# A feed-forward layer's norms, closings and second-product operands, moved and split into smaller steps

## The chip, the core and the metric

The kernel runs on one core of a Trainium2 chip. The metric is the time of one execution on the device, in microseconds; smaller is better. TensorE is called PE here, VectorE DVE, ScalarE ACT, GpSimd POOL, and SyncE SP; SP issues all DMAs.

## The reference

One layer of a hybrid encoder over two sequences, 1024 and 512 tokens of width 1024, in float32: a feed-forward block, a mixer (Hyena convolutions and retention), and a second feed-forward block. Both feed-forward blocks are

```python
h = rmsnorm(x, pre_g)
x = x + 0.5 * rmsnorm((silu(h @ w1) * (h @ w3)) @ w2, post_g)
```

with `rmsnorm(x, g) = x * rsqrt(mean(x * x) + 1e-6) * g` over the 1024 features and an inner width of 2816. Only these two blocks are touched by the change; the mixer between them is not.

## The kernel before

**Layout.** Activations lie transposed, features on the 128 partitions and tokens along the free dimension. The 1536 tokens are two halves `g` of 768, each half two quarters `th` of 384. The 1024 features are two groups `kh` of four blocks of 128. A *quad* is a tile of 128 x 4 x 384: one feature group of one quarter. Quads come from a pool `Y` of 20 slots, and operands of the first product also from a pool `X` of 6.

**Split products.** Every float32 operand is split into a high part (`hi_act`, L58, a copy on ACT to the matmul's format) and a low part (`lo`, L61, a subtraction on DVE). `mm3` (L64) then issues three matmuls (L67 to L69). Both feed-forward products use seven block products in place of eight (a Strassen form over `kh` and `th`).

**First product.** `up_unit` (L265) makes one of 22 blocks of 128 inner features for both quarters: four weight tiles of 256 KB by DMA into a ring of five (`raw`), sums of them on DVE (`s0` to `s3`), seven products of 12 matmuls each into three banks (`ua`, `ub`, `uc`), 84 matmuls a block; split weights sit in a ring of ten (`fw`, L279). ACT copies the first bank to `p1` (L291) before the same bank takes the next product, and applies Silu. The results are the `hid` quads, 12 of them by the end. The moving operands (`self.b`, L263) are split once for each half in `operands` (L241); eight of their quads stay in `Y` for the whole first product.

**Second product.** `down` (L336) runs seven forms `p` over `hid`, each in three parts `c` of four, four and three blocks. For each block it makes the moving operand (`bs`, `xh`, `xl`, L357 to L369: a sum of two `hid`, its high and low parts, or a whole quad at once where the form has a single term), loads 256 KB of weights (L370), splits them and issues 48 matmuls, 12 for each of four banks. After a form its banks are added into the four `z` quads (`ev`, L343). The weights of five forms are sums of two blocks of `w2`; `weight_sums` (L321) forms them beforehand in 20 steps (two loads, an add on DVE, a store to `ws`).

**Norms.** `normed` (L215) loads a quarter's two quads, and `sum_sq` (L185) squares them on ACT and adds them up on DVE to `acc`. `rstd3` (L200) sums over partitions with six instructions on PE (`ss`, L205) and takes the reciprocal root: one DVE operation (L94), a power on POOL (L95), four DVE operations (L96 to L100). `spread` (L208) transposes the result into a bank (`rps`, L212). Then eight `scalar_tensor_tensor` on DVE (L233) multiply by the norm weight (one for each partition) and by `rps`. For the second feed-forward's first half the root is not computed there but read from a row that the mixer left (`rq`, L228).

**Closing.** `post_quads` (L399) does the same for the result `z`, eight multiplies on DVE (L413), then adds the input (`res`, loaded at L411) in pairs of blocks (L415) and stores (L416). In the first feed-forward it then sums the squares of the new values and stores their root to a row for the mixer (L418 to L422).

**Order.** Steps that run beside the products are generators. `ahead` (L455) is the norm of half 1 and the weight sums; it runs beside the 22 blocks of half 0. The closing of half 0 runs beside the blocks of half 1. `ffn` (L424) takes steps only between blocks:

```python
                    self.up_unit(w13[f], [hid[fh, th][c][:, i] for th in range(2)])
                    if f:
                        run(beside, 2 if g or f % 2 else 1)
```

and takes all that are left at block 19. In half 1 the closing takes a step after each part of form 6, the last; its remaining steps (`self.rest`) run beside the mixer's first product or, in the second feed-forward, at the kernel's end. The source order is not the order on the engines: the program is laid out by a planner which, by its own model of time, gives each engine the earliest-written instruction that it takes to be ready, and which makes a tile wait until its slot is free. Each engine then runs its instructions strictly in that order.

Of the kernel before, what the change touches and what calls it, by code (L numbers as in the profile page):

```python
# [46 lines left out]
class Kern:  # L47
# [137 lines left out]
    def sum_sq(self, xs, pool):  # L185

        nc = self.nc
        acc = self.half("acc")
        for i, x in enumerate(xs):
# [3 lines left out]
            if i:  # L193
                nc.vector.tensor_tensor(acc, sq[:, 0], acc, ALU.add)
                nc.vector.tensor_tensor(acc, sq[:, 1], acc, ALU.add)
            else:
                nc.vector.tensor_tensor(acc, sq[:, 0], sq[:, 1], ALU.add)
# [16 lines left out]

    def normed(self, src, gi, pool, row, xs):  # L215
# [6 lines left out]
        if row is None:  # L222
            acc = self.sum_sq(xs, pool)
            yield
            r = self.spread(self.rstd3(acc))
        else:
            r = self.half("rq")
            nc.sync.dma_start(r, row.broadcast_to([128, 384]))  # L228
        yield
        for kh in range(2):  # L230
            for k in range(4):
                g = self.gains[:, gi, 4 * kh + k:4 * kh + k + 1]
                nc.vector.scalar_tensor_tensor(xs[kh][:, k], xs[kh][:, k], g, r, ALU.mult, ALU.mult)  # L233
# [7 lines left out]
    def operands(self, load, X, Y):  # L241
# [3 lines left out]
        b = {}  # L245
        h11, h12 = load(0, 0), load(0, 1)
        b["11"] = self.split(X, h11, "b11")
# [17 lines left out]
    def up_unit(self, w13, hid):  # L265
# [36 lines left out]
        tt(u3, bb, p1, ALU.add)  # L302
        product(bc, s[0], "t1", True)
# [32 lines left out]
    def down(self, w2, hid, Y, z, order):  # L336
# [15 lines left out]
        for p in order:  # L352
            old = {7: 1, 6: 3}.get(p)
            (a, *am), (b, *bm) = self.FORMS[p]
            ps = banks[p] = banks[old] if old else [self.bank("dn") for _ in range(4)]
            for c in range(3):
                n = 4 if c < 2 else 3  # L357
                xh, xl = self.quad(Y, "xh", F32R), self.quad(Y, "xl", F32R)
                if not bm:
                    self.hi_act(xh[:, :n], hid[b][c][:, :n])  # L360
                    self.lo(nc.vector, xl[:, :n], hid[b][c][:, :n], xh[:, :n])
                for i in range(n):
                    f = 4 * c + i
                    if bm:
                        t = self.half("bs")
                        tt(t, hid[b][c][:, i], hid[bm[0]][c][:, i], ALU.add if bm[1] > 0 else ALU.subtract)
                        self.hi_act(xh[:, i], t)
                        self.lo(nc.vector, xl[:, i], t, xh[:, i])
                    raw = self.fr.tile([128, 512], F32, tag="raw", name="raw2")  # L369
                    nc.sync.dma_start(raw, self.ws[p][f // 3][:, f % 3 * 512:f % 3 * 512 + 512] if am else w2[a[0], a[1]][:, f * 512:f * 512 + 512])  # L370
                    wh = self.fw.tile([128, 4, 128], F32R, tag="w", name="w2h")
                    wl = self.fw.tile([128, 4, 128], F32R, tag="w", name="w2l")
                    raw = raw.rearrange("p (m c) -> p m c", c=128)
                    self.hi_act(wh, raw)
                    self.lo(nc.vector, wl, raw, wh)
                    for m in range(4):
                        self.mm3(ps[m], wh[:, m], wl[:, m], xh[:, i], xl[:, i], f == 0 and not old, f == 10, old is not None)
                if c < 2:
                    yield p, c
# [19 lines left out]
    def post_quads(self, z, src, dst, gi, Y, row, g, ths=(0, 1)):  # L399
# [3 lines left out]
        for th in ths:  # L403
            acc = self.sum_sq([z[0, th], z[1, th]], Y)
            yield
            r = self.spread(self.rstd3(acc, True))
            yield
            for mh in range(2):
                t = z[mh, th]
                o = self.quad(Y, "res")  # L410
# [839 lines left out]
```

## Time and profile before

| | |
|---|---|
| median of 3 executions | 3393.17 us (3390.63 to 3396.44) |
| profiled execution: time | 3399.09 us |
| its span, first to last instruction | 3397.3 us |
| mean granted TensorE clock | 0.959 of full speed |
| busy: PE, DVE, ACT, POOL | 91%, 78%, 42%, 16% |
| instructions | 46267, of which 16792 matmuls |
| DMA | 485 MB, 143 GB/s over the span |

The first feed-forward takes the span's first 1110 us: its half 0 about 32 to 572 us, its half 1 to 1072 us. The mixer follows to about 2347 us, and the second feed-forward to the end, its half 0 from 2357 to about 2902 us. A busy share is of the whole span. A row of the timeline or of a group gives an engine's instructions, their busy time, and in brackets or behind the bar the idle time of that engine just before them with what ended it.

### The profile page before, as it was taken

How to read it: one execution, taken by the hardware profiler on the slowest of the kernel's cores; microseconds unless marked ns; L12 is line 12 of the kernel's file. 1: busy time of each engine (PE TensorE's matmuls, PEld its weight loads, DVE VectorE, ACT ScalarE, POOL GpSimd, SP SyncE). 2: the span in 40 equal slices, each digit the busy share in tenths (PEclk: the TensorE clock that was granted, in tenths of full speed). 3: DMA queues.
4: the chain of work that ended last, by engine and by line, in shares of the span. 5: the costliest groups of instructions: out<-in, count | busy, mean ns of one | idle time of the engine just before them, and what ended most of it. 6: DMA issues, size and time to landing. Idle time of an engine off the chain costs nothing. (4 is left out here: it accounts for less than half of the span.)

```text
span 3397.3 us, 46267 instructions
## 1 busy us (share of the span) xinstructions
PE 3087.7 (91%) x16792; PEld 2885.7 (85%) x16792; DVE 2644.2 (78%) x4316; ACT 1431.3 (42%) x2373; POOL 555.3 (16%) x400
## 2 busy tenths in 40 slices
PE   5999998999897799989897998984899999999996
PEld 4999998999897677767676887763899999999996
DVE  8788788777877599678655878886888788877776
ACT  4333464333444234355543344332433455333453
POOL 0000000000200323365322544552000000000000
PEclk8999999999998899999998999997999999999998
DMA  3567454322344534453453125454377544422343
GB/s 128 211 232 286 123 156 143 84 72 75 103 131 139 169 117 160 150 172 112 120 173 128 44 83 172 153 172 139 127 266 272 190 147 134 143 72 72 87 128 131
DMA packets 218806, 485.34 MB, mean 143 GB/s; under 512 B 36432, under 2 KB 64464, under 8 KB 216400
## 3 DMA queue, kind: packets, MB, share of 16 engines
q1 hardware_dynamic: 218576, 482.37, 43.3%
q8 instruction: 132, 2.16, 0.3%
q14 instruction: 98, 0.80, 0.1%
HBM read 382.60 MB, written 99.65 MB: 142 GB/s over the span
## 5 line engine op out<-in xcount | busy, mean ns | idle before, releaser
L68 PE MATMUL dn<-xl,w2h 128*128 128x384 f32 x1232 | 414.8, 337 | 12.7 <-DVE xl L62 12.7
L59 ACT ACTIVATE wh<-raw 128x512 fp32r<-128x512 f32 (+1 forms) x312 | 216.6, 694 | 446.0 <-PE ua L68 96.4
L59 ACT ACTIVATE wh<-s 128x512 fp32r<-128x512 f32 x352 | 221.7, 631 | 427.7 <-PE ua L68 122.3
L69 PE MATMUL dn<-xh,w2l 128*128 128x384 f32 x1232 | 392.4, 337 | 0.0
L67 PE MATMUL dn<-xh,w2h 128*128 128x384 f32 x1232 | 386.8, 337 | 1.7 <-ACT xh L59 1.6
L59 ACT ACTIVATE w2h<-raw 128x512 fp32r<-128x512 f32 (+1 forms) x348 | 236.6, 682 | 342.4 <-PE dn L68 214.9
L62 DVE TENSOR_TENSOR wl<-s,wh 128x512 fp32r<-128x512 f32 x352 | 241.8, 688 | 168.5 <-PE ub L68 84.2
L95 POOL TENSOR_TENSOR r<-m,mhalf 128x3 f32<-128x3 f32 (+1 forms) x35 | 38.8, 1108 | 1847.8 <-DVE m L94 1846.9
L62 DVE TENSOR_TENSOR w2l<-raw,w2h 128x512 fp32r<-128x512 f32 (+1 forms) x316 | 219.5, 705 | 126.0 <-ACT w2h L59 107.7
L67 PE MATMUL wips<-hh,wh 128*128 128x512 f32 x576 | 231.9, 403 | 17.7 <-ACT wh L59 16.7
L68 PEld LDWEIGHTS dn<-xl,w2h 128*128 128x128 f32 x1232 | 232.5, 189 | 15.3 <-DVE xl L62 15.3
L67 PEld LDWEIGHTS dn<-xh,w2h 128*128 128x128 f32 x1232 | 229.5, 189 | 3.8 <-ACT xh L59 3.3
L69 PE MATMUL wips<-hh,wl 128*128 128x512 f32 x576 | 230.7, 401 | 1.8 <-POOL wl L62 1.2
L68 PE MATMUL wips<-hl,wh 128*128 128x512 f32 x576 | 230.8, 401 | 0.0
L69 PEld LDWEIGHTS dn<-xh,w2l 128*128 128x128 f32 x1232 | 230.5, 189 | 0.0
L62 DVE TENSOR_TENSOR wl<-raw,wh 128x512 fp32r<-128x512 f32 (+1 forms) x276 | 199.0, 721 | 39.9 <-ACT wh L59 37.9
L67 PE MATMUL fw<-th,mh 128*128 128x256 f32 x448 | 132.3, 297 | 30.9 <-DVE spec L839 18.2
L67 PEld LDWEIGHTS wips<-hh,wh 128*128 128x128 f32 x576 | 110.4, 192 | 46.3 <-ACT wh L59 17.6
L67 PE MATMUL ua<-b11h,wh 128*128 128x384 f32 x352 | 123.7, 351 | 26.6 <-ACT b11h L59 26.6
L69 PEld LDWEIGHTS wips<-hh,wl 128*128 128x128 f32 x576 | 110.3, 192 | 30.0 <-POOL wl L62 2.4
L68 PE MATMUL fw<-tl,mh 128*128 128x256 f32 x448 | 132.3, 296 | 1.3 <-DVE tl L62 1.2
L69 PE MATMUL fw<-th,ml 128*128 128x256 f32 x448 | 130.1, 291 | 3.8 <-POOL ml L62 3.0
(342 smaller groups left out, 9088.9 us busy)
## 6 DMA issues: line engine op xcount, KB each, us to landing
raw<-ffn_w SPq DMA_DIRECT2D x440, 256.0 KB, 2.7
raw<-ws SPq DMA_DIRECT2D x220, 256.0 KB, 2.6
wsum<-ffn_w SPq DMA_DIRECT2D x60, 768.0 KB, 7.5
raw<-w_in_f SPq DMA_DIRECT2D x48, 512.0 KB, 4.3
ws<-wsum SPq DMA_DIRECT2D x30, 768.0 KB, 4.2
xq<-x SPq DMA_DIRECT2D x16, 768.0 KB, 7.2
res<-x SPq DMA_DIRECT2D x16, 768.0 KB, 6.3
raw<-w_out SPq DMA_DIRECT2D x24, 512.0 KB, 3.4
```

The source lines that it names most:

```text
L59: self.nc.scalar.activation(hi, src, AF.Copy)
L62: eng.tensor_tensor(lo, src, hi.bitcast(F32), ALU.subtract)
L67: mm(ps, lhsT=ah, rhs=bh, start=first, stop=False, **kw)
L68: mm(ps, lhsT=ah, rhs=bl, start=False, stop=False, **kw)
L69: mm(ps, lhsT=al, rhs=bh, start=False, stop=last, **kw)
L95: nc.gpsimd.tensor_tensor(r, m, self.mhalf[:, :n], ALU.pow)
```

## The change

The gains of a norm are multiplied in by eight copies on ACT, in place, before the root is known (`gained`); DVE then multiplies by the root alone, a quad (norms) or half a quad (closings) at a time. Sum, root and spread of a norm or closing are steps of their own, and `up_unit` takes one step in its middle (`mid`) and `ffn` one at its end. At the start both quarters' sums, roots and spreads are issued before either is scaled, and the first quarter's first operand is split before the second quarter is scaled. `down` makes the moving operand of a part one part ahead. In half 1 the closing starts one part earlier, at the end of form 5, the sum of squares of `z[0, 1]` is made after the first part of form 6, and a closing's `res` is loaded with its sum.

```diff
@@ -182,17 +182,19 @@
     def half(self, name):
         return self.ft.tile([128, 384], F32, tag="t", name=name)
-    def sum_sq(self, xs, pool):
-
-        nc = self.nc
-        acc = self.half("acc")
+    def sum_sq(self, xs, pool, acc=None):
+
+        nc = self.nc
+        first = acc is None
+        if first:
+            acc = self.half("acc")
         for i, x in enumerate(xs):
             sq = self.quad(pool, "sq")
             nc.scalar.activation(sq, x, AF.Square)
             nc.vector.tensor_tensor(sq[:, 0:2], sq[:, 0:2], sq[:, 2:4], ALU.add)
-            if i:
+            if i or not first:
+                nc.vector.tensor_tensor(sq[:, 0], sq[:, 0], sq[:, 1], ALU.add)
                 nc.vector.tensor_tensor(acc, sq[:, 0], acc, ALU.add)
-                nc.vector.tensor_tensor(acc, sq[:, 1], acc, ALU.add)
             else:
                 nc.vector.tensor_tensor(acc, sq[:, 0], sq[:, 1], ALU.add)
         return acc
@@ -211,6 +213,12 @@
         for t in range(3):
             self.nc.tensor.transpose(ps[:, t * 128:(t + 1) * 128], r[:, t:t + 1].broadcast_to([128, 128]), self.ident)
         return ps
+
+    def gained(self, xs, gi):
+
+        for i in range(8):
+            x = xs[i // 4][:, i % 4]
+            self.nc.scalar.activation(x, x, AF.Copy, scale=self.gains[:, gi, i:i + 1])
     def normed(self, src, gi, pool, row, xs):
@@ -222,15 +230,17 @@
         if row is None:
             acc = self.sum_sq(xs, pool)
             yield
-            r = self.spread(self.rstd3(acc))
+            self.gained(xs, gi)
+            r = self.rstd3(acc)
+            yield
+            r = self.spread(r)
         else:
+            self.gained(xs, gi)
             r = self.half("rq")
             nc.sync.dma_start(r, row.broadcast_to([128, 384]))
         yield
-        for kh in range(2):
-            for k in range(4):
-                g = self.gains[:, gi, 4 * kh + k:4 * kh + k + 1]
-                nc.vector.scalar_tensor_tensor(xs[kh][:, k], xs[kh][:, k], g, r, ALU.mult, ALU.mult)
+        for x in xs:
+            nc.vector.tensor_tensor(x, x, r.unsqueeze(1).broadcast_to([128, 4, 384]), ALU.mult)
     def split(self, pool, src, name):
         h, l = self.quad(pool, f"{name}h", F32R), self.quad(pool, f"{name}l", F32R)
@@ -238,13 +248,14 @@
         self.lo(self.nc.vector, l, src, h)
         return h, l
-    def operands(self, load, X, Y):
+    def operands(self, load, X, Y, first=None):
         tt = self.nc.vector.tensor_tensor
-        b = {}
+        b = first or {}
         h11, h12 = load(0, 0), load(0, 1)
-        b["11"] = self.split(X, h11, "b11")
+        if not first:
+            b["11"] = self.split(X, h11, "b11")
         t1 = self.quad(Y, "t1")
         tt(t1, h12, h11, ALU.subtract)
         yield
@@ -262,7 +273,7 @@
         b["22"] = self.split(Y, h22, "b22")
         self.b = b
-    def up_unit(self, w13, hid):
+    def up_unit(self, w13, hid, mid):
         nc = self.nc
@@ -300,6 +311,7 @@
         product(bb, s[2], "t3", False)
         u3 = self.half("u3")
         tt(u3, bb, p1, ALU.add)
+        mid()
         product(bc, s[0], "t1", True)
         tt(u3, bc, u3, ALU.add)
         product(bb, a22, "t4", False)
@@ -349,34 +361,44 @@
                 else:
                     tt(z[q][:, m], z[q][:, m], ps[m], ALU.add if sign > 0 else ALU.subtract)
-        for p in order:
+        def moving(p, c):
+            _, (b, *bm) = self.FORMS[p]
+            n = 4 if c < 2 else 3
+            xh, xl = self.quad(Y, "xh", F32R), self.quad(Y, "xl", F32R)
+            if not bm:
+                self.hi_act(xh[:, :n], hid[b][c][:, :n])
+                self.lo(nc.vector, xl[:, :n], hid[b][c][:, :n], xh[:, :n])
+            for i in range(n if bm else 0):
+                t = self.half("bs")
+                tt(t, hid[b][c][:, i], hid[bm[0]][c][:, i], ALU.add if bm[1] > 0 else ALU.subtract)
+                self.hi_act(xh[:, i], t)
+                self.lo(nc.vector, xl[:, i], t, xh[:, i])
+            return xh, xl
+
+        parts = [(p, c) for p in order for c in range(3)]
+        ahead = moving(*parts[0])
+        for j, (p, c) in enumerate(parts):
             old = {7: 1, 6: 3}.get(p)
-            (a, *am), (b, *bm) = self.FORMS[p]
-            ps = banks[p] = banks[old] if old else [self.bank("dn") for _ in range(4)]
...
-                if c < 2:
-                    yield p, c
+            a, *am = self.FORMS[p][0]
+            if c == 0:
+                ps = banks[p] = banks[old] if old else [self.bank("dn") for _ in range(4)]
+            xh, xl = ahead
+            for i in range(4 if c < 2 else 3):
+                f = 4 * c + i
+                raw = self.fr.tile([128, 512], F32, tag="raw", name="raw2")
+                nc.sync.dma_start(raw, self.ws[p][f // 3][:, f % 3 * 512:f % 3 * 512 + 512] if am else w2[a[0], a[1]][:, f * 512:f * 512 + 512])
+                wh = self.fw.tile([128, 4, 128], F32R, tag="w", name="w2h")
+                wl = self.fw.tile([128, 4, 128], F32R, tag="w", name="w2l")
+                raw = raw.rearrange("p (m c) -> p m c", c=128)
+                self.hi_act(wh, raw)
+                self.lo(nc.vector, wl, raw, wh)
+                for m in range(4):
+                    self.mm3(ps[m], wh[:, m], wl[:, m], xh[:, i], xl[:, i], f == 0 and not old, f == 10, old is not None)
+            if j + 1 < len(parts):
+                ahead = moving(*parts[j + 1])
+            if c < 2:
+                yield p, c
+                continue
             if p == 1:
                 ev((1, 1), ps, True)
             elif p == 4:
@@ -401,17 +423,20 @@
         nc = self.nc
         for th in ths:
-            acc = self.sum_sq([z[0, th], z[1, th]], Y)
+            acc = self.sum_sq([z[1, th]], Y, z["sum"]) if th and "sum" in z else self.sum_sq([z[0, th], z[1, th]], Y)
+            os = [self.quad(Y, "res") for _ in range(2)]
+            for mh in range(2):
+                nc.sync.dma_start(os[mh], src[mh][th])
+            self.gained([z[0, th], z[1, th]], gi)
             yield
-            r = self.spread(self.rstd3(acc, True))
+            r = self.rstd3(acc, True)
+            yield
+            r = self.spread(r)
             yield
             for mh in range(2):
-                t = z[mh, th]
-                o = self.quad(Y, "res")
-                nc.sync.dma_start(o, src[mh][th])
-                for k in range(4):
-                    nc.vector.scalar_tensor_tensor(t[:, k], t[:, k], self.gains[:, gi, 4 * mh + k:4 * mh + k + 1], r, ALU.mult, ALU.mult)
+                t, o = z[mh, th], os[mh]
                 for k in range(0, 4, 2):
+                    nc.vector.tensor_tensor(t[:, k:k + 2], t[:, k:k + 2], r.unsqueeze(1).broadcast_to([128, 2, 384]), ALU.mult)
                     nc.vector.tensor_tensor(t[:, k:k + 2], t[:, k:k + 2], o[:, k:k + 2], ALU.add)
                     nc.sync.dma_start(dst[mh][th][:, k:k + 2], t[:, k:k + 2])
             if row is not None:
@@ -446,10 +471,14 @@
         with pool("xq", 6, side=side) as X, pool("fs", side=side) as self.fs, pool("ft", 6, side=side) as self.ft, \
                 pool("fw", 10, side=side) as self.fw, pool("fr", 5, side=side) as self.fr, pool("pm", 8, space=PSUM) as self.pm:
             h = [], []
-            for th in range(2):
-                for _ in ready(0, th, h[th]):
-                    pass
-            for _ in self.operands(lambda kh, th: h[th][kh], X, Y):
+            steps = [ready(0, th, h[th]) for th in range(2)]
+            for _ in range(1 if row_in else 3):
+                for step in steps:
+                    next(step)
+            run(steps[0], 9)
+            first = {"11": self.split(X, h[0][0], "b11")}
+            run(steps[1], 9)
+            for _ in self.operands(lambda kh, th: h[th][kh], X, Y, first=first):
                 pass
             def ahead():
@@ -477,9 +506,9 @@
                     for th in range(2):
                         if i == 0:
                             hid.setdefault((fh, th), []).append(self.quad(Y, "hid"))
-                    self.up_unit(w13[f], [hid[fh, th][c][:, i] for th in range(2)])
+                    self.up_unit(w13[f], [hid[fh, th][c][:, i] for th in range(2)], lambda: run(beside, 1 if f else 0))
                     if f:
-                        run(beside, 2 if g or f % 2 else 1)
+                        run(beside, 1)
                 z = {}
                 post_of = self.post_quads(z, srcs[g], dsts[g], post, Y, row_out, g)
                 if g == 0:
@@ -491,7 +520,9 @@
                     beside = post_of
                 else:
                     for p, c in self.down(w2, hid, Y, z, (1, 4, 7, 2, 3, 5, 6)):
-                        if p == 6:
+                        if (p, c) == (6, 0):
+                            z["sum"] = self.sum_sq([z[0, 1]], Y)
+                        if p == 6 or (p, c) == (5, 2):
                             run(post_of)
         self.rest = post_of
```

## Rows read from the trace of the kernel before

**Rows 1.** The page, busy time, share of the span, instructions; PE.

```profile
PE 3087.7 (91%) x16792; PEld 2885.7 (85%) x16792; DVE 2644.2 (78%) x4316; ACT 1431.3 (42%) x2373; POOL 555.3 (16%) x400
```

**Rows 2.** Busy time by stretch: PE, PEld, DVE, ACT, POOL, PEclk, DMA share, GB/s.

```profile
60.00:130.00 70.00, 59.46 (x319) 59.06 (x318) 53.89 (x101) 25.30 (x40) 2.34 (x2) 0.88 0.41 143
130.00:345.00 215.00, 215.00 (x1240) 214.87 (x1240) 183.61 (x287) 82.86 (x149) 0.00 (x0) 1.00 0.73 269
...
560.00:630.00 70.00, 56.23 (x301) 54.99 (x300) 60.84 (x116) 27.34 (x39) 3.40 (x3) 0.88 0.42 140
...
870.00:930.00 60.00, 49.63 (x259) 48.06 (x258) 47.72 (x74) 26.13 (x48) 17.00 (x8) 0.91 0.40 114
...
2395.00:2460.00 65.00, 53.19 (x291) 52.44 (x290) 51.19 (x97) 24.23 (x37) 1.97 (x2) 0.92 0.42 153
...
2895.00:2945.00 50.00, 45.20 (x263) 43.88 (x262) 48.02 (x92) 18.91 (x31) 2.92 (x2) 1.00 0.53 190
```

**Rows 3.** Waits of PE over the span: us in total, times, longest.

```profile
PE ss L205 <- DVE acc L195: 52.1, 8, 13.4
PE rps L212 <- DVE r L100: 33.7, 10, 4.8
...
PE dn L68 <- DVE xl L62: 12.7, 8, 4.2
```

**Rows 4.** Timeline, first feed-forward, closing of half 0: ACT and PE.

```profile
588.15 4.23 ACT L191 ACTIVATE sq<-z 128x1536 f32<-128x1536 f32 x3 [0.86 <-DVE z L415]
...
592.28 0.47 ACT L291 ACTIVATE p<-ua 128x384 f32<-128x384 f32 x1
...
592.81 0.69 PE L67 MATMUL ua<-b21h,wh 128*128 128x384 f32 x1 [7.78 <-ACT p L291]
```

**Rows 5.** Groups by shape, ACT: a copy with a scale per partition, one without, Square.

```profile
L837 ACT ACTIVATE spec<-fw,turn 128x256 f32<-128x256 f32 x104 | 42.1, 475 | 58.7 <-PE fw L69 58.4
L291 ACT ACTIVATE p<-ua 128x384 f32<-128x384 f32 x88 | 41.8, 475 | 20.7 <-PE ua L69 20.7
...
L191 ACT ACTIVATE sq<-z 128x1536 f32<-128x1536 f32 x24 | 34.8, 1478 | 41.1 <-DVE z L415 29.2 <-DVE z L350 10.3 <-issue 1.5
```

**Rows 6.** Timeline, start of the first feed-forward: PE and DVE.

```profile
26.57 1.44 PE L205 MATMUL ss<-ones,acc 128*128 128x1 f32 x6 [6.04 <-DVE acc L195]
...
32.19 4.29 DVE L233 SCALAR_TENSOR_TENSOR xq<-xq,gains,rps 128x384 f32<-128x384 f32 x8 [0.99 <-PE rps L212]
...
36.39 1.75 DVE L249 TENSOR_TENSOR t<-xq 128x1536 f32<-128x1536 f32 x1
```

**Rows 7.** Timeline, start of the second feed-forward: ACT and DVE.

```profile
2346.76 0.63 ACT L59 ACTIVATE wh<-raw 128x512 fp32r<-128x512 f32 x1 [22.77 <-DMA x<-z]
...
2353.47 8.55 DVE L233 SCALAR_TENSOR_TENSOR xq<-xq,gains,rq 128x384 f32<-128x384 f32 x16 [3.55 <-DMA rq<-row]
```

**Rows 8.** Timeline, the kernel's end: PE and DVE.

```profile
3369.91 2.12 DVE L350 TENSOR_TENSOR z<-z,dn 128x384 f32<-128x384 f32 x4 [1.87 <-PE dn L69]
...
3371.27 0.49 PE L212 MATMUL rps<-ident,r 128*128 128x128 f32 x3
3371.94 4.28 DVE L413 SCALAR_TENSOR_TENSOR z<-z,gains,rps 128x384 f32<-128x384 f32 x8
...
3377.01 0.95 DVE L192 TENSOR_TENSOR sq<-sq 128x768 f32<-128x768 f32 x1
...
3381.07 0.56 DVE L195 TENSOR_TENSOR acc<-sq,acc 128x384 f32<-128x384 f32 x1
...
3381.68 1.44 PE L205 MATMUL ss<-ones,acc 128*128 128x1 f32 x6 [9.93 <-DVE acc L195]
...
3390.25 3.56 DVE L415 TENSOR_TENSOR z<-z,res 128x768 f32<-128x768 f32 x4
```

**Rows 9.** Timeline, end of the first feed-forward: PE.

```profile
1084.48 1.44 PE L205 MATMUL ss<-ones,acc 128*128 128x1 f32 x6 [12.52 <-DVE acc L195]
```

**Rows 10.** Busy time in the stretch with the most DMA, columns as in rows 2.

```profile
250.00:280.00 30.00, 30.00 (x175) 30.00 (x174) 26.66 (x41) 11.65 (x22) 0.00 (x0) 1.00 0.99 374
```

More of the change, by code (lines that the diff above doesn't have):

```diff
@@ L350, in ev @@
                     tt(z[q][:, m], z[q][:, m], ps[m], ALU.add if sign > 0 else ALU.subtract)
-        for p in order:
-            old = {7: 1, 6: 3}.get(p)
-            (a, *am), (b, *bm) = self.FORMS[p]
-            ps = banks[p] = banks[old] if old else [self.bank("dn") for _ in range(4)]
[L356 to L377, printed above, removed]
-                if c < 2:
-                    yield p, c
```

## The prediction

> **What bounds the kernel now.** I read four views in this order: the page's busy shares, the busy time by stretch, the waits of PE, and the timeline round the longest of them. The page shows TensorE busy for 91% of the span [rows 1], which says little by itself. The stretches tell more [rows 2]. From 130 to 345 us, the products of a feed-forward half, PE is busy 215.00 of 215.00 us with 1240 matmuls: 215 / 1240 = 0.1734 us each, and nothing beside it can make that faster. DVE is at 85% there and ACT at 39%. So only what PE loses in the other stretches can be won: idle time, and matmuls that ran slowly after idle time. The mean granted clock is 0.88 in 60 to 130 us, where PE had been idle, and 1.00 in 130 to 345 us; 2.4 GHz is the upper of its two levels, 1.2 GHz the lower. A stretch's slow part is its busy time less its matmuls at 0.1734 us.
>
> The waits name the causes [rows 3]: 52.1 us for the sum of squares (`acc`), 33.7 us for the reciprocal root (`r`), 12.7 us for `xl`; the timeline adds one of 7.78 us for ACT's copy of a bank [rows 4]. The first two are chains of a few short instructions that PE, in its fixed order, stands still for, because the sum, the root and the spread follow each other within one block.
>
> All terms below are against the profiled execution, 3399.1 us (span 3397.3); it lies 5.9 us above the median of the runs, 3393.2, so I take the sum off the median.
>
> **Part 1, norms of the second half under the first half's products: -25 us.** The two stretches are 60 to 130 and 2395 to 2460 us. Idle: 70 - 59.46 = 10.5 and 65 - 53.19 = 11.8 us. Slow: 59.46 - 319 x 0.1734 = 4.1 and 53.19 - 291 x 0.1734 = 2.7 us [rows 2]. After the change sum, root and spread are half a block apart: 84 matmuls a block, 42 x 0.1734 = 7.3 us. PE's longest wait for `r` is 4.8 us [rows 3], so 7.3 us of products cover it. Bounds: 0 to -29.1. I take all but 1.5 us of idle time in each, with the slow part in proportion: -19.3 - 5.8 = -25, nearest to the full end, because the cover is longer than any of the `r` waits.
>
> **Part 2, closing of the first half under the second half's products: -14 us.** In 560 to 630 us, 13.8 us idle and 56.23 - 301 x 0.1734 = 4.0 us slow; in 2895 to 2945 us, 4.8 us idle [rows 2]. The first has two causes. PE stood 7.78 us for `p<-ua` on ACT, which was queued behind three Squares of 4.23 us that in turn waited for the closing's adds on DVE [rows 4]. The rest is mostly the wait for `r`. The steps' new distance removes the latter; of the former half stays, since the row sum still puts two Squares of 1.48 us each on ACT behind DVE's adds [rows 5]. So -13.8 + 3.9 + 1.0 = -9, slow -2, and -3.5 in the second stretch. Bounds: 0 to -22.6.
>
> **Part 3, operands of the second product one part ahead: -11 us.** All 12.7 us of waits for `xl` [rows 3] are at the start of a part, where copy and subtraction were issued together with the matmuls that need them. A part earlier they have 4 x 12 x 0.1734 = 8.3 us of matmuls as cover. Bounds: 0 to -12.7, and up to -4.7 for the slow matmuls in 870 to 930 us (49.63 - 259 x 0.1734). That stretch also holds the mixer's first norm, which crowds DVE (10.4 us idle in all), so I take -10 and -1. The first part of each product has no part before it to hide in and gains nothing.
>
> **Part 4, the two beginnings: -8 us.** In the first, both halves' sums now stand ahead of the first scaling. The second half's `acc` waited for it (PE idle 6.04 us), so its chain moves up by about the eight multiplies, 4.29 us, and each half's eight multiplies become two of the kind that took 1.75 us, pitch about 1.67: 4.29 - 3.35 = 0.9 [rows 6]. That makes -5; bounds 0 to -9. In the second feed-forward the 16 multiplies took 8.55 us on the path to the product on `t2h` [rows 7]; four of 1.67 us take 6.7, so -1.9, and the split that now stands between the halves lets fill-in work of other matmuls slip past: -3 (bounds 0 to -6). The 16 new copies on ACT fall into 22 us in which it was idle [rows 7].
>
> **Part 5, the two ends: -10 us.** At the kernel's end the first half's spread came after the last matmul, at 3371.27; then DVE worked 8 multiplies (4.28 us) and the first adds before the second half's sum, and PE's `ss` came 9.93 us late, at 3381.68 [rows 8]. After the change the spread is one part earlier, 3 x 12 x 0.1734 = 6.2 us: it ends at about 3365.7. The second half's sum needs only its second quarter. From there DVE has 8 operations of the pitch of the adds (3.56 / 4 = 0.89 us), 7.1 us, the four evacuations (2.12 us) and 0.95 + 2 x 0.55 us of sums [rows 8]: about 3377.0 instead of 3381.68, -4.7; and the last scale with its adds is 7.1 us instead of 4.28 + 3.56, -0.7. So -5.4. At the first feed-forward's end `ss` is 12.52 us late for the same reason [rows 9]; its gain is capped by the mixer's first weights, which stand behind the stores in SP's queue: I take -4.5, a little under the other end. Bounds together 0 to -16.
>
> **What it adds: +8 us.** (a) 64 copies a feed-forward on ACT, each with a weight per partition. No such row of 384 columns exists; 256 columns with one took 475 ns, 384 without 475 ns [rows 5]. From 1478 ns for 1536 columns the price is (1478 - 475) / 1152 = 0.87 ns a column, so 475 + 128 x 0.87 = 586 ns, an estimate; 64 make 38 us on an engine 61% idle. Hidden, if they don't stand before a bank's copy: 0 to +28 (second rival); +4. In place of them DVE loses little: eight multiplies at 4.29 us become two at 3.35, and in the closings four at 0.89. (b) The weight sums (20 a feed-forward, three moves of up to 786 kB each) now run two a block instead of 1.5, since steps are taken twice in every block: 0 to +79 (last rival); +4. (c) The weights' loads and `res` are issued earlier and hold two more of the 20 slots: nothing, as 8 slots of operands and 4 to 8 of `hid` leave at least 4 free then.
> A rule of the Trainium skill speaks against (a): ScalarE: Activation LUTs, Rules for kernel authors, sends `mul` to VectorE, not ScalarE. Here DVE is the fuller engine by 85% to 39% [rows 2], so the trace speaks for the move. By that page (What ACT_TABLE_LOAD costs: 280 ns + 0.833 ns a column, 93 ns of overlap) a copy would cost 0.51 us, an estimate, and the sum would be the same.
>
> **Sum:** -25 - 14 - 11 - 8 - 10 + 8 = -60; 3393.2 - 60 = about 3333.
>
> **Rivals.**
> - **The planner puts them together again.** The order on each engine is made by its own clock, and it places a spread as soon as it thinks `r` ready. For it: at present it has PE wait although matmuls are at hand. Against it: in 2895 to 2945 us most waits are short. Parts 1 and 2 then give nothing: -11 - 8 - 10 + 8 = -21, 3372. Chance 0.16, of which 0.04 that no difference shows.
> - **ACT's queue.** Eight copies of up to 0.586 us behind two Squares are 7.6 us in a row; PE can spare ACT's bank copy for two products, 24 x 0.1734 = 4.2 us. If the rest, 3.5 us, is paid in eight steps (two norms and two closings in each feed-forward), that is +28 where I count +4: 3357. For it: exactly this queue cost 7.78 us [rows 4]. Against it: the copies are ready long before. Chance 0.15.
> - **Slower: the DMA queue.** Two sums a block move 2 x 2.16 MB (mean of full and short ones) and 1.05 MB of weights in 14.6 us, 368 GB/s. The densest stretch reached 374 at a share of 0.99, with PE still busy throughout [rows 10]; the average was 269 [rows 2]. If only 290 can be held and the weights of the products wait behind the sums, each of ten blocks in both feed-forwards takes 5.37 MB / 290 GB/s = 18.5 us, +3.9 x 20 = +79: 3333 + 75 = 3408. It decides below 368 GB/s. Against it: the sums can slip into four further blocks. Chance 0.11.
>
> **How the numbers follow.** The sum has 0.58. All parts at their full ends give 3393 - 103 = 3290 without new costs; the range starts at 3302, since not all will, and ends at 3377 to hold the first two rivals; it leaves out the last. Within 0.2% (7 us, about what a measurement of this kernel can tell from no change) has 0.04, faster 0.58 + 0.15 + 0.12 = 0.85, slower 0.11.
>
> **What would show it.** Right: in 60 to 130 and 2395 to 2460 us PE is busy over 95% at a clock near 1.00; the waits for `r` drop below 10 us and for `xl` below 3; the last `ss` comes some 5 us earlier after the last matmul. Wrong: PE waits for `p<-ua` in several blocks (ACT's queue), or ACT waits for `raw<-ffn_w` (DMA), or `rps` still follows `ss` with idle time before it (the planner).

## The result and the profile after

The changed kernel takes 3358.8 us (median of 4 runs, 3357.1 to 3364.5) beside 3394.8 us for the kernel before: a ratio of 0.990 (0.988 to 0.992), 36 us less. It lies inside the forecast range (3302 to 3377) and on the forecast side, but the forecast gain was 60. The profiled execution has a span of 3355.3 us, 42.0 less than the one before; that one lay some 4 us above its runs and this one some 2 below, so the working below is against 42.

First the page's busy times of the changed kernel, then its busy time by stretch (columns as in rows 2) and PE's waits. The second feed-forward's first matmul comes 31.0 us earlier than before (2326.2 for 2357.2), so the stretch that was 2395 to 2460 us is now 2364 to 2429.

```profile
PE 3086.6 (92%) x16792; PEld 2890.0 (86%) x16792; DVE 2622.8 (78%) x4236; ACT 1495.7 (45%) x2501; POOL 552.8 (16%) x400
```

```profile
60.00:130.00 70.00, 65.58 (x367) 64.89 (x366) 59.08 (x102) 36.27 (x62) 2.32 (x2) 0.95 0.45 154
130.00:345.00 215.00, 210.75 (x1200) 210.42 (x1199) 178.14 (x278) 80.29 (x144) 0.00 (x0) 0.98 0.74 272
560.00:630.00 70.00, 64.43 (x356) 63.73 (x355) 65.99 (x119) 34.45 (x54) 4.94 (x3) 0.93 0.40 128
2364.00:2429.00 65.00, 60.00 (x337) 59.31 (x337) 53.59 (x93) 34.58 (x59) 2.41 (x2) 0.95 0.46 161
```

```profile
PE ss L207 <- DVE acc L197: 46.9, 8, 15.2
...
PE ub L67 <- DVE u L313: 12.7, 8, 3.5
PE rps L214 <- DVE r L100: 9.8, 3, 5.7
...
PE ub L67 <- ACT wh L59: 8.7, 3, 4.3
...
PE dn L68 <- DVE xl L62: 6.4, 2, 4.2
```

Against rows 2, the norm and closing stretches are fuller (367 matmuls in 60 to 130 us for 319, 337 in the later norm stretch for 291), but 130 to 345 us, which had been full, now lacks 4.25 us of PE and 40 matmuls. Against rows 3, the wait for `r` fell from 33.7 to 9.8 us and for `xl` from 12.7 to 6.4; the one of 7.78 us for ACT's copy [rows 4] is gone; the wait for `acc` hardly moved, 52.1 to 46.9.

**Where the time went.** The same matmul can be found in every trace by its place in its bank's order, so the spans between such marks can be compared. "Norms" is from the first matmul of a feed-forward to the 121st on `ua` (five blocks on); "sums" from there to the first `dn`; "closings" six blocks from the first `ua` of half 1; "end 1" from there to the mixer's first projection; "mixer" to the second feed-forward's first matmul; "end 2" from the sixth block of half 1 to the kernel's end; "other" the start and the products of half 0. Both feed-forwards are added. Each number is the difference to the kernel before, in us, one execution each; the labels are those of the experiments.

| kernel | norms | sums | closings | end 1 | end 2 | other | mixer | span | span less mixer |
|---|---|---|---|---|---|---|---|---|---|
| changed | -17.7 | +13.8 | -13.2 | -16.5 | -4.0 | -5.2 | +0.9 | -42.0 | -42.9 |
| changed, again (e9) | -17.7 | +13.8 | -13.2 | -14.9 | -4.0 | -5.3 | +2.8 | -38.5 | -41.4 |
| e1, stores on GpSimd | -16.1 | +17.0 | -14.2 | -17.1 | -4.0 | -5.2 | -3.8 | -43.4 | -39.5 |
| e2, sums at 1.5 a block | -17.7 | -0.1 | -13.0 | -15.7 | -3.6 | -1.5 | +7.1 | -44.4 | -51.5 |
| e3, operands not ahead | -20.3 | +13.8 | -15.5 | -1.9 | +6.9 | -1.5 | -6.6 | -25.3 | -18.6 |
| e4, gains on DVE | -12.1 | +13.5 | -5.5 | -13.3 | -2.2 | -4.9 | +8.6 | -15.9 | -24.5 |
| e5, root and spread joined | -7.4 | +14.8 | -7.9 | -9.1 | -3.9 | -1.0 | -6.7 | -21.1 | -14.4 |
| e6, old start | -17.4 | +14.5 | -13.1 | -11.3 | -5.6 | -1.0 | +12.9 | -21.0 | -33.9 |
| e7, old end | -17.1 | +14.1 | -13.2 | -2.3 | -5.1 | -5.1 | +2.8 | -26.1 | -28.9 |
| e8, e2 and one step more | -30.0 | +2.0 | -13.7 | -17.1 | -3.5 | -5.1 | -9.3 | -76.7 | -67.4 |
| e10, e8 and apply in two | -29.0 | +2.6 | -9.4 | -17.3 | -3.5 | -5.2 | -2.0 | -63.8 | -61.8 |
| e11, sums on GpSimd | -16.9 | +44.5 | -15.8 | -17.6 | -5.3 | -2.1 | -0.7 | -13.8 | -13.2 |
| e12, step without e2 | -29.1 | +2.0 | -12.9 | -14.5 | -4.0 | -2.2 | +11.1 | -49.6 | -60.7 |

Three things stand out. The changed kernel wins 57 us outside the mixer and gives 13.8 back in "sums". The mixer, whose code nothing touches, moves by up to 13 us. And a second product can run at one of two paces without any wait, as the same 140 us of the changed kernel and of e2 show:

```profile
390.00:530.00 140.00, 140.00 (x810) 140.00 (x809) 123.29 (x198) 87.98 (x149) 0.00 (x0) 1.00 0.51 151
```

```profile
390.00:530.00 140.00, 140.00 (x795) 140.00 (x793) 119.26 (x189) 84.55 (x142) 0.00 (x0) 1.00 0.48 149
```

Between marks, 132 matmuls take 22.88 us in the one and 23.32 in the other, 3.1 us for a whole second product. In the first feed-forward, half 0 has the slower pace in e2, e5, e6, e11 and e12 and half 1 in e2, e6, e7, e10 and e12; what sets it was not found. So 3 us in "other" or "end 1" need not be an edit's. The experiments take the sums first, then the parts.

### The profile page after: what moved, and what is told of

Read it like the earlier page. It is cut to its first block, busy times and chain, and to the rows that moved or that the text cites. A ratio compares the mean times of both kernels' runs of the same rounds, so it can differ in the third digit from the quotient of the medians.

```text
span 3355.3 us, 46275 instructions
## 1 busy us (share of the span) xinstructions
PE 3086.6 (92%) x16792; PEld 2890.0 (86%) x16792; DVE 2622.8 (78%) x4236; ACT 1495.7 (45%) x2501; POOL 552.8 (16%) x400
## 5 line engine op out<-in xcount | busy, mean ns | idle before, releaser
L67 PE MATMUL dn<-xh,w2h 128*128 128x384 f32 x1232 | 402.5, 337 | 1.7 <-ACT xh L59 1.6
L69 PE MATMUL dn<-xh,w2l 128*128 128x384 f32 x1232 | 401.3, 336 | 0.0
L67 PE MATMUL wips<-hh,wh 128*128 128x512 f32 x576 | 232.8, 404 | 18.6 <-DVE vo L781 9.0
L67 PEld LDWEIGHTS wips<-hh,wh 128*128 128x128 f32 x576 | 110.9, 192 | 48.1 <-ACT wh L59 11.7
L67 PE MATMUL ub<-t2h,wh 128*128 128x384 f32 x352 | 121.5, 345 | 16.7 <-ACT wh L59 8.7
L68 PEld LDWEIGHTS wips<-hl,wh 128*128 128x128 f32 x576 | 110.7, 192 | 29.4 <-POOL hl L62 2.9
```

Of the source, the lines that this page charges most:

```text
L67: mm(ps, lhsT=ah, rhs=bh, start=first, stop=False, **kw)
L68: mm(ps, lhsT=ah, rhs=bl, start=False, stop=False, **kw)
L69: mm(ps, lhsT=al, rhs=bh, start=False, stop=last, **kw)
```

## The experiments

Each kernel ran in three timed rounds beside the kernel before; ratios are to it. All start from the changed kernel unless said.

**What the lost 13.8 us are.** The timeline of the changed kernel, DVE, SP, ACT and PE, round the stall:

```profile
169.69 0.56 DVE L318 TENSOR_TENSOR p<-ub,p 128x384 f32<-128x384 f32 x1 [3.02 <-PE ub L69]
...
170.16 1.75 DVE L344 TENSOR_TENSOR wsum<-wsum 128x1536 f32<-128x1536 f32 x1
...
171.94 0.33 SPq L345 DMA_DIRECT2D ws<-wsum  x1
172.29 0.69 DVE L310 TENSOR_TENSOR s<-raw 128x512 f32<-128x512 f32 x1
...
174.07 1.52 SPq L284 DMA_DIRECT2D raw<-ffn_w  x2
174.51 0.69 DVE L304 TENSOR_TENSOR s<-s,raw 128x512 f32<-128x512 f32 x1
...
175.98 0.69 PE L67 MATMUL ub<-t2h,wh 128*128 128x384 f32 x1 [4.25 <-ACT wh L59]
```

PE has run out of split weights. They come from additions on DVE (L310, L304), which stand after an evacuation that waits for PE itself (L318) and after a weight sum (L344); SP had stood at the store of that sum. PE waits in the same way from 2473.4 us on. After each stall the granted clock is down for a while: 0.79 in 174 to 190 us, 0.80 in 2476 to 2492.

e1, the stores of the weight sums moved from SP's queue:

```diff
-                nc.sync.dma_start(self.ws[p][c][:, :512 * n], ts[0])
+                nc.gpsimd.dma_start(self.ws[p][c][:, :512 * n], ts[0])
```

> Only the stores of the weight sums move, from SP's queue to GpSimd's. Theory Q (queue order): PE's waits of 4.25 us at 171.7 and 4.29 us at 2473.4 come from weights' loads that stood behind such a store on SP, which stood idle 9.04 and 9.25 us for a sum on DVE; they go, with the slow matmuls after them: 3358.8 - 14 = about 3345. Theory B (bandwidth): the transfers had filled the DMA engines (share 0.99 from 150 to 168 us), whichever queue issues the stores: both waits stay, 3359 within 3.

Measured: 3357.4 us, 0.989 (0.987 to 0.990), "sums" +17.0. The first wait of the same matmul is still there:

```profile
177.11 0.69 PE L67 MATMUL ub<-t2h,wh 128*128 128x384 f32 x1 [3.12 <-ACT wh L59]
```

Theory Q falls: SP at the store was not what held the weights back.

e2, the density of before:

```diff
-                yield from self.weight_sums(w2, Y)
+                for i, _ in enumerate(self.weight_sums(w2, Y)):
+                    yield
+                    if i % 3 == 2:
+                        yield
```

> Weight sums three in four steps, so 1.5 a block as in the kernel before; all else as changed. Theory D (density made the stall, by the queue or by bandwidth): both waits of PE for a weight at 171.7 and 2473.4 us go, about 3345. Theory O (an accident of the planner's order, whatever the density): a wait of about 4 us stays or appears elsewhere, 3359 within 4.

Measured: 3354.6 us, 0.988 (0.986 to 0.989). Both waits are gone, "sums" is -0.1 and the stretch is full again:

```profile
130.00:345.00 215.00, 215.00 (x1241) 215.00 (x1240) 181.60 (x285) 82.88 (x148) 0.00 (x0) 1.00 0.75 275
```

The 13.9 us are won inside the feed-forwards, as theory D has it; the total shows 2 to 4 of them, since the mixer took 6.2 more and "other" 3.7, of which 3.1 are the slower pace of half 0.

e11, the additions of the weight sums taken off DVE:

```diff
-                nc.vector.tensor_tensor(ts[0], ts[0], ts[1], ALU.add if more[1] > 0 else ALU.subtract)
+                nc.gpsimd.tensor_tensor(ts[0], ts[0], ts[1], ALU.add if more[1] > 0 else ALU.subtract)
```

> The changed kernel with the 40 additions of the weight sums on GpSimd, which is idle there, instead of DVE; loads and stores as they are. Theory V (the late weights come from DVE's order: the next unit's additions stood behind a product's evacuation and a weight sum of 1.75 us, at 172.29 although their data had landed by 167.5): the waits of 4.25 us at 171.7 and 4.29 at 2473.4 go, -13 inside the feed-forwards, 3346 with some 10 of scatter from the mixer. Theory B (the burst of transfers makes the weights late, 9 to 12 us from issue to landing): both waits stay within 1 us, 3359 with the same scatter.

Measured: 3385.7 us, 0.998 (0.997 to 0.999). Both waits stay (3.12 and 3.64 us), so the weight sum on DVE did not make them. The rest of theory V is not refuted: the additions still stand after the evacuation that waits for PE.

```profile
177.47 0.56 DVE L318 TENSOR_TENSOR p<-ub,p 128x384 f32<-128x384 f32 x1 [3.13 <-PE ub L69]
...
178.60 0.69 DVE L310 TENSOR_TENSOR s<-raw 128x512 f32<-128x512 f32 x1
```

Many short waits come beside the two. The groups of DVE in 130 to 345 us, of the changed kernel and then of e11, show why:

```profile
L62 DVE TENSOR_TENSOR wl<-s,wh 128x512 fp32r<-128x512 f32 x57 | 39.2, 689 | 16.8 <-ACT wh L59 8.5 <-PE ub L68 7.5 <-ACT hid L309 0.6
```

```profile
L62 DVE TENSOR_TENSOR wl<-s,wh 128x512 fp32r<-128x512 f32 x52 | 58.2, 1122 | 15.1 <-PE ub L68 7.7 <-ACT wh L59 6.9 <-PE uc L68 0.3
...
L313 DVE TENSOR_TENSOR u<-ub,p 128x384 f32<-128x384 f32 x13 | 7.2, 553 | 6.6 <-PE ub L69 6.6
```

**What the norms still lacked.** The timeline of the changed kernel, ACT, DVE and PE, first norm under the products:

```profile
67.40 1.49 ACT L193 ACTIVATE sq<-xq 128x1536 f32<-128x1536 f32 x1 [0.45 <-DMA xq<-x]
...
69.32 2.13 ACT L221 ACTIVATE xq<-xq,gains 128x384 f32<-128x384 f32 x4
...
71.35 1.47 ACT L193 ACTIVATE sq<-xq 128x1536 f32<-128x1536 f32 x1
...
75.87 0.55 DVE L197 TENSOR_TENSOR acc<-sq,acc 128x384 f32<-128x384 f32 x1
...
76.56 1.41 PE L207 MATMUL ss<-ones,acc 128*128 128x1 f32 x6 [4.22 <-DVE acc L197]
```

From the first Square to `acc` the chain takes 76.42 - 67.40 = 9.0 us, with four gains copies between the Squares; half a block is 7.3.

e8, e2's edit and one more half block between sum and `ss` (the start takes four steps for three):

```diff
             acc = self.sum_sq(xs, pool)
             yield
+            yield
             self.gained(xs, gi)
...
-            for _ in range(1 if row_in else 3):
+            for _ in range(1 if row_in else 4):
```

> Weight sums at 1.5 a block, and one more half block between the sum of squares of a norm and the matmuls that add it up. With the change that chain takes 9.0 us (first Square at 67.40, acc at 76.42) where half a block is 7.3. Theory C (the chain is longer than its distance): PE's waits for acc of 4.2 us in each feed-forward go with their slow matmuls, -8 beside the -13 that the density gives inside the feed-forwards; with the mixer's scatter of some 6 us, 3331 to 3348. Rival M (the planner puts the sum's matmuls where its clock has acc ready, whatever the step): waits stay at 4 us: 3345 to 3356.

Measured: 3327.3 us, 0.980 (0.978 to 0.982), 66 us below the kernel before. Both waits for `acc` are gone, and the "norms" gain 30.0 where the change gained 17.7:

```profile
60.00:130.00 70.00, 68.54 (x397) 67.30 (x396) 58.52 (x105) 38.45 (x66) 1.70 (x2) 1.00 0.43 149
```

Theory C holds. This version beats both kernels; of its 34.7 us of span on the changed one, 12.3 are the norms, 11.8 the sums, 10.2 the mixer. The mixer's share is why it came out below theory C's 3331.

e12, the same step at the change's two sums a block (e8 without e2's edit):

> The changed kernel with one more half block between a norm's sum of squares and the matmuls that add it up, at the change's two weight sums a block. Theory C (chain longer than its distance, separate from the density): PE's waits for acc of 4.2 us under the first products go and each such stretch gains 5 to 7, but PE's waits for a weight of 4.2 us stay: 3347 with some 10 of scatter from the mixer. Rival D (with the norms' steps taking one block more, the sums come one block later and the waits for weights go with it): 3334 with the same scatter.

Measured: 3349.7 us, 0.988 (0.986 to 0.990). The norms gain as in e8 (-29.1), and the waits for weights are gone as well, "sums" +2.0: rival D. So density alone does not decide. From SP's DMA issues the sum loads that stand ahead of a block's weights can be counted: in the changed kernel twelve between 130.2 and 151.0 us, and the weights issued next, from 153.7 to 159.0, land 11.7 to 9.3 us later (2.7 in the median over the span; the last of the four could not be told); in e2 ten by 144.7 and the next at 175.2; in e12 eight by 142.6 and the next at 169.9; in the kernel before ten by 154.2. The stall comes with the burst of twelve. Whether the late landing (166.7 us for the third) or the planner's place for the additions (172.29) cost more of it was not separated. Two readings lean to the place: DVE stood idle for 3.02 us before the evacuation at 169.69, three of the four loads having landed; and in the kernel before a load issued at 147.4 us landed 11.7 us later while PE stayed busy.

**What the parts of the change are worth.** e5, root and spread in one step (last closing begins with form 6):

```diff
-            r = self.rstd3(acc)
-            yield
-            r = self.spread(r)
+            r = self.spread(self.rstd3(acc))
...
-                        if p == 6 or (p, c) == (5, 2):
+                        if p == 6:
```

(the same join in the closing, and two steps for three at the start)

> Root and spread in one step again (and the last closing begins a part later, as before); two steps a block stay, so the weight sums keep their density. Theory R (the prediction's: half a block between root and spread covers the wait for r): PE's waits for r, 9.8 us with the change, return to some 25 to 30; the stretches 60 to 130, 560 to 630, 2380 to 2460 and 2880 to 2940 lose about 15 together, the two ends about 8: 3358.8 + 23 = 3382. Theory M (the planner sets the order by its own clock, and what gained there is DVE's relief by the copies on ACT): waits for r stay near 10, only the ends lose: 3359 to 3367.

Measured: 3377.1 us, 0.994 (0.992 to 0.996). PE's waits for `r` are 20.0 us against 9.8, norms and closings lose 10.3 and 5.3 us: 15.6 together, as theory R said, though its 25 to 30 us of waits were not reached.

e4, `gained` not called, eight multiplies by weight and root on DVE as before:

```diff
-                    nc.vector.tensor_tensor(t[:, k:k + 2], t[:, k:k + 2], r.unsqueeze(1).broadcast_to([128, 2, 384]), ALU.mult)
+                    for q in range(k, k + 2):
+                        nc.vector.scalar_tensor_tensor(t[:, q], t[:, q], self.gains[:, gi, 4 * mh + q:4 * mh + q + 1], r, ALU.mult, ALU.mult)
```

(likewise in the norms)

> Norm weights and reciprocal root in one operation on DVE again, no copies on ACT; steps as changed. Theory A (the copies stand between the Squares on ACT and so delay the sums): PE's waits for the first acc of each second half (4.22 us at 72.3, 4.26 us at 2374.0) fall to about 2, and the first ss at the start comes 1.8 us earlier: 3352 to 3356. Theory H (the copies are hidden, and DVE pays for the multiplies): 3359 to 3364.

Measured: 3383.1 us, 0.996 (0.994 to 0.997). Both theories fall. Without the copies everything beside them is worse: norms by 5.6, closings by 7.7, ends by 5.0; 18.4 us outside the mixer. By what way is not shown: DVE's busy time is only 10.4 us longer (2633.2 us, 2622.8 in the changed kernel), and the planner's order is another one too.

e3, operands made with their own part:

```diff
-        ahead = moving(*parts[0])
...
-            xh, xl = ahead
+            xh, xl = moving(p, c)
...
-            if j + 1 < len(parts):
-                ahead = moving(*parts[j + 1])
```

> Operands of the second product issued again with their own part. Theory P (the term of the prediction, -11): PE's waits for xl return to about 12 us and the four products lose some 9 to 11 us: 3368 to 3370. Theory N (the gain at these places came from the norms' and closings' other order, the operands were hidden anyway): 3359 within 3.

Measured: 3373.3 us, 0.993 (0.992 to 0.995). The total is near theory P's, but outside the mixer 24.3 us are lost, and at another place: at the ends (14.6 and 10.9 us), where the early closing's sum now waits 9.47 and 9.50 us instead of 1.69:

```profile
1040.87 1.44 PE L207 MATMUL ss<-ones,acc 128*128 128x1 f32 x6 [9.47 <-DVE acc L197]
```

e7, the closing of half 1 begun one part later, without the early sum:

```diff
-                        if (p, c) == (6, 0):
-                            z["sum"] = self.sum_sq([z[0, 1]], Y)
-                        if p == 6 or (p, c) == (5, 2):
+                        if p == 6:
```

> Only the early closing at the two ends is undone (its first step one part later, no early sum of the second half). Theory E (the earlier closing gave what the ends gained, 5.2 us of wait for ss at the first, 3.5 at the second): 3358.8 + 9 = 3368. Rival G (the copies on ACT gave it, as in the run with gains on DVE the ends' waits are 12.67 and 10.12 us): 3359 to 3362.

Measured: 3373.3 us, 0.993 (0.991 to 0.995). The first end loses 14.2 us, 3.1 of them by the slower pace of half 1. PE's wait before the mixer's first projection is 22.9 us (16.0 in the kernel before, 9.0 in the changed one). The kernel's end gains 1.1: what the second sum wins there, the early `ss` takes. Theory E for the one, rival G for the other.

e6, the old order at the two starts:

```diff
-            for _ in range(1 if row_in else 3):
-                for step in steps:
-                    next(step)
-            run(steps[0], 9)
-            first = {"11": self.split(X, h[0][0], "b11")}
-            run(steps[1], 9)
+            for step in steps:
+                run(step, 9)
```

> Halves one after the other at both beginnings again. Prediction: the two beginnings lose 5 and about 1: 3365. Rival, from the trace of the change, where the first product starts 0.6 us earlier than before: the order is worth under 2: 3359 to 3361.

Measured: 3377.6 us, 0.994 (0.993 to 0.996), worse than either theory; but the first start and the norms account for 1.4 of the 21.0 us of span, the slower pace in both halves of the first feed-forward for some 6, and the mixer for 12.0, of which the second start is 3.6. That raised the question of the next run.

e9, the changed kernel unedited:

> The changed kernel, unedited. The mixer, whose code no edit touches, took 1211 to 1233 us from its first projection to the next feed-forward in the ten profiles so far. Theory O (each edit gives the planner another order there): here it takes 1221.5 within 3 again, total about 3359. Theory X (chance of the single execution): it falls anywhere in that range, total 3349 to 3371.

Measured: 3361.8 us, 0.990 (0.988 to 0.992). The mixer takes 1223.3 us (1221.4 before), and every mark of the first feed-forward up to 1084 us comes within 0.4 us of the first profile. That speaks for theory O: the mixer's scatter, 1211 to 1233 us, comes with the planner's order. PE's order there is another one in every kernel but e1 and e11, which have the same on every engine, and their mixers take 1216.7 and 1219.8 us. Two such pairs are few, and chance has a share: the timed executions of e2 alone lie between 3346.7 and 3360.7 us.

e10, e8 with the closing's last step in two:

```diff
             for mh in range(2):
+                if mh and not (g and th):
+                    yield
```

> The kernel with the extra half block and 1.5 weight sums a block; in addition a closing's last step (scale, add, store) is two steps, one for each pair of tiles. Theory C (PE's 3.46 us wait for u at 571.0 comes from the closing's burst on DVE): it falls under 1, -5 with slow matmuls in that stretch, the total 3322 with some 7 of scatter from the mixer. Rival K (the burst is the row sum's adds, not the closing's): the wait stays, total 3327 with the same scatter.

Measured: 3335.1 us, 0.982 (0.981 to 0.984). The first closing lost 6.2 us against e8, the second won 1.8, and PE's wait there is 3.02 us (3.46 in e8), so by that sign it is rival K. In the first closing a wait of 2.17 us for `r`, at 605.55 us, is new; why the two closings differ stays open.

## Why the prediction came out as it did

The forecast -60 and the measured -42 of the profiled executions, by the terms of the sum:

| term | forecast | measured |
|---|---|---|
| Part 1, norms | -25 | -17.7 |
| Part 2, closings | -14 | -13.2 |
| Parts 3 and 5, operands ahead and ends | -21 | -25.1 (-4.6 half 0, -16.5, -4.0) |
| Part 4, first start | -5 | -0.6 |
| Part 4, second start (last `fw` matmul to first `ua`) | -3 | -3.5 (141.4 to 137.9) |
| rest of the mixer's span | 0 | +4.4 |
| weight sums' density | +4 | +13.8 |
| copies on ACT | +4 | in the rows above |

- **Part 1 was mis-sized at "7.3 us of products cover it".** It priced the longest wait for `r` and then struck out the stretch's whole idle time, of which more than a third was the wait for the sum (3.5 of 10.5 and 4.9 of 11.8 us). The waits for `r` in these stretches did go; the chain of the sum, 9.0 us, is longer than half a block, and 4.2 us of idle time with its slow matmuls stayed in each. With one half block more (e8, e12) the norms give -29 to -30, about the bound of -29.1 that the prediction had worked out, of which 2.0 come back in the blocks behind ("sums"). The clock rose only part of the way: 0.95 in both stretches for 0.88 and 0.92, with PE busy for 94% and 92%, so the sign that it had named for being right (over 95%, near 1.00) did not come; in e8 it did, 98% at 1.00 in 60 to 130 us.
- **The density term was mis-sized.** It was seen, and its price put at +4 with a rival of +79 for a queue that can't keep up. What came was one burst with one stall of 4.2 us in each feed-forward and slow matmuls behind it, 13.8 together; it is gone in e2 and e12.
- **The copies on ACT had the wrong sign.** They were given a cost, and DVE "loses little". e4 says that they are worth 18 us, so part of what was booked to steps and distances in Parts 1 and 2 is theirs: of the 30.9 us, 15.6 are lost without the distance (e5) and 13.3 without the copies (e4), each taken out alone. A copy takes 605 ns, where the estimate was 586. The Trainium skill (ScalarE: Activation LUTs, Rules for kernel authors) sends multiplications to VectorE; here, with DVE the fuller engine, e4 decides against it.
- **Part 2's number held** (-9.9 and -3.3 by closing, for -11 and -3.5), its account only in part: e4 puts 7.7 us on the copies, e5 5.3 on the distance. The queue for ACT's bank copy did not come back: no wait for `p` is left, so the second rival, whose 3357 lies nearest to the result, was not what happened. Nor was the first: e5 shows that the distance did act.
- **Part 3** gave 3.7 of the 4.6 in half 0, where e3 loses them again at the waits for `xl`; the other 0.9 is the slower pace that the kernel before has in the first 264 matmuls of the first feed-forward's half 0. Its larger share is at the ends, which the prediction did not link to it: without it, the earlier closing's sum waits 9.5 us (e3). The two waits for `xl` that are left, 4.2 and 2.3 us where under 3 in all was to show the prediction right, lie in the product that shares DVE with the mixer's first norm, which the prediction had named as crowded. They were as long before the change, and the reading that all such waits are at the start of a part was wrong for them: they are at the fourth block of a first part and the third of a second. (The layout's 48 matmuls a block, 12 for each bank, are those of a part of four blocks; a block has 12, three for each bank, as the prediction's 4 x 12 takes it.)
- **Part 4, first start:** the sums do stand first, and the second quarter's `ss` comes 3.8 us earlier (22.74 us), near the forecast 4.29. But the first quarter's came later, at 15.24 us, since the gains copies stand between the Squares, and the second root's last DVE operation comes at 30.43 us, 4.6 us after POOL had its power, with the first quarter's scaling and split in between; the first product starts 0.6 us earlier. e6 puts the order at about 1.
- **Part 5:** at the kernel's end the wait for the last `ss` fell by 3.5 us, not 4.7, and the early `ss`, with a wait of 1.69 us and slow matmuls after it, cost more: the last product takes 166.9 us with it and 162.7 without (e7). The early closing gains nothing there (-5.1 without it, -4.0 with it); without the copies -2.2 are left (e4). At the first end the gain was far larger than the -4.5, because PE waited 7.0 us less before the mixer's first projection too; which transfer let it go was not traced.
- **The total.** That it lies inside a range of 75 us says little for the terms: the ends gave 4 us more than was booked, the norms lacked 7, the first start and the untouched mixer 4 each, and the density took 10 more. That Part 2 fits to 1 us is luck, since the copies made over half of it. The parts' full ends add up to 100 us, not 103; nothing hangs on it.

## What to carry to other kernels

Before a step is moved under other work, lay the whole chain of that step (sum, root, spread, each with its queue) against the distance it gets, not the longest of its waits: a chain of 9.0 us under 7.3 us of products still stalled, and one half block more gave 12 us. When steps are taken more often, look at what else is taken with them, here the loads of the weight sums. Where a planner sets the order, read gains by stretch between marks of the same instruction: the kernels here moved an untouched stage by up to 13 us.

## What the runs showed of the hardware

An addition on GpSimd holds DVE up rather than slowing it. With the weight sums there (3632 ns for 1536 columns, against 1753 on DVE), DVE's subtraction `wl` went from 689 to 1122 ns in the mean, while its operations that read a PSUM bank stayed at 553. The mean hides two kinds:

```profile
161.19 3.72 POOL L344 TENSOR_TENSOR wsum<-wsum 128x1536 f32<-128x1536 f32 x1 [9.99 <-DMA wsum<-ffn_w]
...
162.35 3.10 DVE L62 TENSOR_TENSOR wl<-raw,wh 128x512 fp32r<-128x512 f32 x1
```

The addition ends at 164.91 us, the subtraction 0.55 later. In 130 to 345 us of e11, 20 DVE operations with both inputs in SBUF began during such an addition, and each ended 0.42 to 0.55 us after it, whenever it had begun; the other 149 took at most 0.69 us. The Trainium skill (SBUF — State Buffer, SBUF: two separate sides) says that DVE and GpSimd share a port pair, which a DVE instruction with two inputs in SBUF contends for, and that whoever comes second waits for the other's end; the rows agree.
